# Rotary half swap on TensorE, first weights split ahead of a load, and squares summed on GpSimd: three edits of a two-block transformer kernel

## The chip, the cores and the metric

The kernel runs on one core of a Trainium2 chip. The metric is the device time of one execution in microseconds (us), lower is better. The core has the engines TensorE (PE, and PEld for its weight loads), VectorE (DVE), ScalarE (ACT), GpSimd (POOL) and SyncE (SP, which issues the DMA transfers).

## The reference, cut to what matters

Two blocks of two layers each work on one sequence of 256 tokens of width 1024, all in float32. The pieces that the change touches:

```python
def rms_norm(x, g):
    y = x32 * lax.rsqrt(jnp.mean(x32 * x32, axis=-1, keepdims=True) + EPS)
    return (y * g).astype(x.dtype)

def apply_rope(x, cos, sin):           # halves of 32 in a head of 64
    x1, x2 = x[..., :half], x[..., half:]
    return concatenate([x1 * c - x2 * s, x2 * c + x1 * s], axis=-1)

# first block, each layer: mod = silu(c) @ w_ada[l] + b_ada[l]
h = rms_norm(x, g_norm1[l]) * (1.0 + sc1) + sh1
u = h @ w_in[l] + b_in[l]              # q_lat, kv_lat, k_rope, ... by columns
# ... latent attention (with rope on a part of q and k), stick-breaking attention
x = x + gt1 * (merged @ w_out[l])
h = rms_norm(x, g_norm2[l]) * (1.0 + sc2) + sh2    # then a gated feed-forward part

# second block, each layer: the same frame; 8 + 8 query heads and 2 + 2 key heads of 64,
# each normed per head and, on the 256 main tokens, rotated by rope; the 256 context
# tokens go through the same projections without rope; then 16 experts of 32 tokens each.
q = apply_rope(rmsnorm(p_q, qg), cos, sin)
x = x + gt1 * latent_mixer(...)        # ends with merged @ w_out
x = x + gt2 * expert_choice_ffn(modulate(rmsnorm(x, g_ffn), sh2, sc2), ...)
```

## The kernel before, in words

Activations lie feature-major: 128 features on the partitions, 256 tokens along the free dimension, eight such tiles for the width of 1024. A float32 product is made of three products of rounded parts: `wsplit` (lines 227 and 228) casts a weight tile to its high part on ScalarE and subtracts to get the low part on VectorE, and `mm3` (line 245) multiplies high by high, high by low and low by high. One 128-column tile of a projection is thus 24 matmuls of 256 columns. Small products (sums over the partitions, attention of the first block) are plain float32 matmuls; on the page each of them is two rows.

The order of the program text is not the order on the engines: a scheduler under the tile framework places each instruction on its in-order engine, and buffers are given out by tags with a fixed number of slots. The PSUM tags are `mm` (2 slots), `dd` (3) and `acc` (3). SP issues all loads of weights in one queue.

What the change and the prediction touch:

- **Start of the program** (`body`, `prep`, `cols1`, `first_layer`). The six parts of the first adaptive vector come from loads of 1 MB of `w_ada`, eight of which are taken by TensorE at the start (line 406). When the last is in, the first norm (lines 483, 491) makes the parts `hh` and `hl`, and the first projection runs on weights of `w_in` (`fm2`, line 245). That first load of `w_in` stands behind the eight of `w_ada`.
- **Norm statistics** (`Stats.add`, line 113). Behind each of the eight 128-feature tiles of an out projection (`out_proj`, line 751 adds the tile to x), ScalarE squares the tile and TensorE adds its sum over the partitions by a float32 matmul with a matrix of ones. In the mixers of the second block a second small matmul (line 116) makes router logits beside it. There are five out projections: two layers of the first block, context and main tokens of the second block's first layer, main tokens of its last.
- **`rsqrt`** (line 303 and around): logarithm and exponential on ScalarE, then one Newton step on VectorE; line 303 makes the scaled input for that step on VectorE.
- **`rope`** (lines 766 to 768): four GpSimd instructions, each on 32 partitions, multiply a quarter by the sines and write it to the other half of its head; VectorE multiplies by the cosines (767) and adds (768). It runs twice in each layer of the first block and ten times in each mixer of the main tokens (two key and eight query tiles), 24 in all, which makes 96 GpSimd rows.
- **`head_norm`** (lines 909 to 917 of the second block's heads): square on ScalarE, scaling by the gain on VectorE (line 910), a float32 matmul with a block matrix (line 912), `rsqrt`, `rope`. Line 926 or 1017 multiplies by the norm, lines 1020 and 1021 split.

The main mixer of a layer runs: keys and values of both branches, four query tiles of branch one, attention of branch one (lines 957 to 985), four query tiles of branch two, attention of branch two, then projections and the out projection, and then the experts (line 1272), whose 192 MB of weights follow in the same load queue.

Of the kernel before, what the change touches and what calls it, by code (L numbers as in the profile page):

```python
# [17 lines left out]
P = 128  # L18
# [28 lines left out]
    [("ident", P), ("slot", 1), ("freq", 1), ("eps", 1), ("halfpi", 1), ("one", 1), ("sign", 1), ("ones", P), ("mask_m", P)],  # L47
# [16 lines left out]
def shape_constants():  # L64
# [8 lines left out]
    c["sign"][:, 0] = sign  # L73
    c["ntri"][:] = -(p[:, None] >= p[None, :]).astype(np.float32)
# [26 lines left out]
class Stats:  # L101
    def __init__(self, kernel, x, bank=None, proj=None):
        self.kernel, self.x, self.ps, self.bank, self.proj = kernel, x, None, bank or kernel.ad, proj

    def add(self, k):
        kn = self.kernel
        if self.ps is None:
            kn.use_table("ln_exp")
            bank = self.bank()
            self.ps, self.pl = bank[:, :S], bank[:, S:2 * S]  # L110
        sq = kn.k1([P, S])
        kn.act(sq, self.x[:, k], AF.Square)
        i = kn.nc.tensor.matmul(self.ps, kn.c("ones"), sq, start=k == 0, stop=k == KT - 1, skip_group_check=True)  # L113
        if self.proj:
            w, e = self.proj
            j = kn.nc.tensor.matmul(self.pl[e], w[:, k], self.x[:, k], start=False, stop=k == KT - 1,
                                    skip_group_check=True)
            if k == 0:
                kn.order(i, j)
# [6 lines left out]
class Kernel:  # L126
# [164 lines left out]
    def rsqrt(self, ps, n, scale, shape=None, out=None):  # L291
# [11 lines left out]
        nc.vector.tensor_scalar(f(v), ps, scale, EPS, op0=OP.mult, op1=OP.add)  # L303
        self.act(y, y, AF.Exp, scale=-0.5)
        nc.vector.tensor_tensor(u, y, y, op=OP.mult)
# [206 lines left out]
    def cols1(self, l):  # L512
# [27 lines left out]
        if l == 0:  # L540
            for r, (n, o, _) in zip(rows, sets):
                self.rows_out(r, n, o)
        yield c1, c2, c3

    def first_layer(self, l, cols, mod, then, r):
# [14 lines left out]
        w = self.wload(w_in, 0, KT, 0, 256)  # L560
        ql = self.k2([P, 2, S])
        pq = self.mm((P, S))
        jobs = [(self.dd(), self.wsplit1(w[:, :, j * P:(j + 1) * P], [P, KT, P])) for j in range(2)]
        self.fm2(jobs, h)
        if l == 0:
            self.const_rest()
        for j in range(2):
# [159 lines left out]
        st = Stats(self, x)  # L727
# [29 lines left out]
    def rope(self, q, n, cos, sin):  # L757
# [6 lines left out]
        for a in range(0, P, 32):  # L764
            src, dst = slice(a, a + 32), slice(a ^ 32, (a ^ 32) + 32)
            nc.gpsimd.tensor_tensor(u[dst], q[src], sin[src], op=OP.mult)  # L766
        nc.vector.tensor_tensor(o, q, cos, op=OP.mult)
        nc.vector.tensor_tensor(o, o, u, op=OP.add)
# [137 lines left out]
    def head_norm(self, ps, g, rot, gain):  # L906
# [3 lines left out]
        nc.vector.tensor_scalar(q, ps, g, gain, op0=OP.mult, op1=OP.mult)  # L910
# [7 lines left out]
    def kv(self, l, s, h, c, kk, vv):  # L918
# [5 lines left out]
        for br, w in enumerate(ws):  # L924
            q, r = self.head_norm(jobs[br][0], c[:, 65 + 2 * br:66 + 2 * br], s == 0, 1.0)
# [73 lines left out]
    def mixer(self, l, s, x, mod, cols, kk, vv, h, side=None, steps=None):  # L999
# [5 lines left out]
        outs = {}  # L1005
        for br in range(2):
            half = [self.wload(w_in, 4 * f, 4, 512 + 512 * br, 512) for f in range(2)]
            q = self.k8([P, 2, 4, S], F32R)
            for mt in range(4):
# [6 lines left out]
                qq, r = self.head_norm(ps, c[:, 64 + 2 * br:65 + 2 * br], s == 0, 0.125)  # L1016
# [77 lines left out]
        st = Stats(self, x, proj=(wr, e))  # L1094
# [320 lines left out]
def body(tc, io, out, consts, n1=DEPTH, n2=DEPTH):  # L1415
    with ExitStack() as ctx:
# [7 lines left out]
        def prep(i):  # L1424
# [7 lines left out]
            if ns == 1:  # L1432
# [77 lines left out]
```

## Time and profile before

| what | value |
|---|---|
| runs | 2777.68, 2778.06, 2783.66 us; median 2778.06 |
| the profiled execution | 2779.97 us, its span 2778.0 us |
| busy share of the span | PE 93%, PEld 66%, DVE 51%, ACT 38%, POOL 5% |
| TensorE clock | 0.976 of full speed on average |
| loads | 742.59 MB, 267 GB/s on average |

The busy share of PE is a mean over stages with different limits. Matmuls are pipelined, so a row's duration is longer than the step to the next row: a 256-column row of line 245 lasts 0.28 us and the next follows 0.117 us later at full clock.

### The profile page before, as it was taken

What the parts mean: (1) busy time and instruction counts of PE and PEld (TensorE: products, weight loads), DVE (VectorE), ACT (ScalarE), POOL (GpSimd) and SP (SyncE); (2) the same over time, 40 slices, a digit from 0 to 9 for tenths busy, and PEclk for the clock granted to TensorE, in tenths of its full rate; (3) what the DMA queues carried; (4) which work ended last, traced back from release to release, by engine and by line L of the source; (5) the groups of instructions that cost most, each with busy time, mean ns of one, the idle gap of its engine ahead of it and who ended that gap; (6) DMA issues with size and microseconds to landing.
All of it is one profiled execution on the core that took longest, in us unless ns stands there. A gap on an engine that the chain in (4) does not pass through costs nothing.

```text
span 2778.0 us, 45247 instructions
## 1 busy us (share of the span) xinstructions
PE 2573.3 (93%) x18732; PEld 1828.8 (66%) x18732; DVE 1409.1 (51%) x2667; ACT 1050.6 (38%) x1986; POOL 132.7 (5%) x155
## 2 busy tenths in 40 slices
PE   7998999999999999889999999999889998878886
PEld 5898998888998689768984333333667994222222
DVE  5989977767778855797552011010598562000001
ACT  3564555555556644556452000001466442000000
POOL 0100000000000000120011000000031001000000
PEclk8999999999999999999999999999999999999998
DMA  8788854677555488423656999999623766999999
GB/s 315 238 317 287 322 175 155 221 281 249 178 193 191 153 272 263 135 76 114 182 179 235 361 410 400 425 379 407 242 77 114 228 220 257 424 425 424 424 425 320
DMA packets 315003, 742.59 MB, mean 267 GB/s; under 512 B 16214, under 2 KB 212782, under 8 KB 275118
## 3 DMA queue, kind: packets, MB, share of 16 engines
q1 hardware_dynamic: 313710, 738.66, 72.0%
q8 instruction: 147, 2.41, 0.3%
q10 hardware_dynamic: 1088, 1.05, 0.1%
q14 instruction: 58, 0.48, 0.1%
HBM read 738.61 MB, written 1.05 MB: 266 GB/s over the span
## 4 chain that ended last, share of the span: by engine, by line
PE 72%; DMA 15%; DVE 8%; ACT 3%; issue 1%; POOL 1%; SPq 1%; DVEq 0%; ACTq 0%; POOLq 0%
PE dd L245 36%; PE acc L1272 11%; PE mm L1272 5%; PE acc L245 3%; DMA k<-in_w_e_down_dram 3%; DMA w<-in_w_e_up_dram 2%; DMA k<-in_w_e_up_dram 2%; DMA w<-in_w_e_down_dram 2%; DMA k<-in_w_e_gate_dram 2%; DMA w<-in_w_e_gate_dram 2%; PE mm L985 2%; PE ad L406 2%; PE ad L113 1%; PE mm L979 1%; DVE wl L228 1%
## 5 line engine op out<-in xcount | busy, mean ns | idle before, releaser
L245 PE MATMUL dd<-hh,wh 128*128 128x256 f32 x2384 | 682.9, 288 | 17.1 <-ACT hh L269 13.6
L228 DVE TENSOR_TENSOR wl<-w,wh 128x1024 fp32r<-128x1024 f32 (+1 forms) x534 | 553.9, 1041 | 270.7 <-ACT wh L227 264.1
L245 PE MATMUL dd<-hh,wl 128*128 128x256 f32 x2384 | 676.9, 285 | 12.7 <-DVE wl L228 12.5
L227 ACT CAST wh<-w 128x1024 fp32r<-128x1024 f32 (+1 forms) x534 | 478.0, 900 | 527.2 <-PE dd L245 389.5
L245 PE MATMUL dd<-hl,wh 128*128 128x256 f32 x2384 | 675.5, 284 | 1.0 <-DVE hl L491 0.8
L245 PEld LDWEIGHTS dd<-hh,wh 128*128 128x128 f32 x2384 | 453.8, 191 | 38.7 <-ACT hh L269 15.1
L245 PEld LDWEIGHTS dd<-hh,wl 128*128 128x128 f32 x2384 | 454.4, 191 | 18.3 <-DVE wl L228 14.7
L245 PEld LDWEIGHTS dd<-hl,wh 128*128 128x128 f32 x2384 | 455.2, 191 | 6.4 <-issue 3.2
L1272 PE MATMUL acc<-w,pt 128*32 128x512 f32 x624 | 222.9, 597 | 30.0 <-DMA w<-in_w_e_up_dram 16.1
L1294 DVE TENSOR_TENSOR wh<-wh,acc 128x512 f32<-128x512 f32 x20 | 13.8, 688 | 450.1 <-PE acc L1272 450.1
L1272 PE MATMUL acc<-k,pt 128*32 128x512 f32 x692 | 224.0, 597 | 8.7 <-DMA k<-in_w_e_up_dram 5.2
L245 PE MATMUL dd<-k,wh 128*128 128x256 f32 x896 | 165.0, 284 | 1.1 <-DVE k L665 0.8
L1272 PE MATMUL acc<-w,k 128*32 128x512 f32 x480 | 160.9, 608 | 0.7 <-ACT pt L1169 0.7
L1272 PE MATMUL acc<-w,wl 128*32 128x512 f32 x396 | 139.8, 600 | 13.9 <-DMA w<-in_w_e_down_dram 13.9
L1272 PE MATMUL acc<-k,wl 128*32 128x512 f32 x432 | 146.7, 600 | 4.6 <-DMA k<-in_w_e_down_dram 4.6
L245 PEld LDWEIGHTS dd<-k,wh 128*128 128x128 f32 x896 | 138.6, 190 | 4.8 <-DVE k L665 1.7
L1272 PE MATMUL acc<-k,k 128*32 128x512 f32 x376 | 133.3, 605 | 0.0
L1272 PEld LDWEIGHTS acc<-w,pt 128*32 128x32 f32 x624 | 45.8, 109 | 131.7 <-issue 69.0
L766 POOL TENSOR_TENSOR k<-k,rope 32x256 f32<-32x256 f32 (+1 forms) x96 | 88.4, 921 | 852.2 <-DVE k L599 460.0
L245 PE MATMUL dd<-k,wl 128*128 128x256 f32 x448 | 126.2, 282 | 2.2 <-DVE wl L228 2.2
L1307 DVE SCALAR_TENSOR_TENSOR x_res<-dd,mod,x_res 128x256 f32<-128x256 f32 x64 | 28.9, 484 | 174.5 <-PE dd L1306 174.4
L1272 PEld LDWEIGHTS acc<-k,pt 128*32 128x32 f32 x692 | 46.3, 109 | 93.7 <-issue 61.6
(357 smaller groups left out, 4444.0 us busy)
## 6 DMA issues: line engine op xcount, KB each, us to landing
w<-in_w_in_dram SPq DMA_DIRECT2D x104, 1024.0 KB
w<-in_w_ada_dram SPq DMA_DIRECT2D x63, 1024.0 KB
w<-in_w_e_gate_dram SPq DMA_DIRECT2D x54, 1024.0 KB
w<-in_w_e_up_dram SPq DMA_DIRECT2D x54, 1024.0 KB
w<-in_w_e_down_dram SPq DMA_DIRECT2D x48, 1024.0 KB
w<-in_w_up_dram SPq DMA_DIRECT2D x44, 1024.0 KB
k<-in_w_e_gate_dram SPq DMA_DIRECT2D x43, 1024.0 KB
k<-in_w_e_down_dram SPq DMA_DIRECT2D x43, 1024.0 KB
```

The source lines that it names most:

```text
L113: i = kn.nc.tensor.matmul(self.ps, kn.c("ones"), sq, start=k == 0, stop=k == KT - 1, skip_group_check=True)
L227: self.nc.scalar.copy(h, src)
L228: self.nc.vector.tensor_tensor(l, src, h.bitcast(F32), op=OP.subtract)
L245: self.last_mm = self.nc.tensor.matmul(ps, a, b, start=first and i == 0, stop=last and i == len(ops) - 1, skip_group_check=group)
L406: nc.tensor.matmul(ad[32 * g:32 * g + 32], cs[:, 2 * c + j], t[:, j, 256 * g:256 * g + 256], start=j == 0 and (c == 0 or not hold), stop=j ...
L766: nc.gpsimd.tensor_tensor(u[dst], q[src], sin[src], op=OP.mult)
L979: nc.tensor.transpose(pp[:, i], e[:, i * P:(i + 1) * P], self.c("ident"))
L985: nc.tensor.matmul(po[64 * f:64 * f + 64], vv[:, kt, P * br + 64 * f:P * br + 64 * f + 64], pt[:, f, i], start=i == 0, stop=i == len(kts) ...
L1272: nc.tensor.matmul(accs[s][n][32 * e:32 * e + 32], lhs(s, 2 * kp + k, e), tiles[e][k][:, 512 * n:512 * n + 512], start=kp == 0 and k == 0, ...
L1294: nc.vector.tensor_tensor(a, a, pu[s][n], op=OP.mult)
L1307: nc.vector.scalar_tensor_tensor(x[:, k], ps, gate[:, k:k + 1], x[:, k], op0=OP.mult, op1=OP.add)
```

## The change

Three edits are joined. First, `rope` makes the swapped halves with one float32 matmul by a signed permutation (`swap`) into a PSUM tile of the tag `mm`, and VectorE multiplies that tile by the sines; GpSimd does nothing there any more. The gain of a head is applied by ScalarE and no longer by VectorE, and so is the scaled input in `rsqrt`. Second, the first load of `w_in` is queued ahead of the eighth load of `w_ada`, and its two column tiles are split right there; the constants and two of three rows of columns change places in the order too. Third, the statistics behind the five out projections (`sums=True`) keep the first and last square as they are, and GpSimd adds squares two to seven into one tile, of which TensorE makes one matmul: three matmuls instead of eight.

```diff
-    [("ident", P), ..., ("ones", P), ("mask_m", P)],
+    [("ident", P), ..., ("ones", P), ("mask_m", P), ("swap", P)],
+    c["swap"][p ^ 32, p] = -1.0
...
 class Stats:
...
-        sq = kn.k1([P, S])
+        if self.sums and k == 1:
+            self.total = sq = kn.t([P, S], "sq", 1)
+        else:
+            sq = kn.k1([P, S])
         kn.act(sq, self.x[:, k], AF.Square)
-        i = kn.nc.tensor.matmul(self.ps, kn.c("ones"), sq, start=k == 0, stop=k == KT - 1, skip_group_check=True)
+        if self.sums and 1 < k < KT - 1:
+            kn.nc.gpsimd.tensor_tensor(self.total, self.total, sq, op=OP.add)
+            sq = self.total
+        if not (self.sums and 0 < k < KT - 2):
+            i = kn.nc.tensor.matmul(self.ps, kn.c("ones"), sq, start=k == 0, stop=k == KT - 1, skip_group_check=True)
...
     def rsqrt(...):
-        nc.vector.tensor_scalar(f(v), ps, scale, EPS, op0=OP.mult, op1=OP.add)
         self.act(y, y, AF.Exp, scale=-0.5)
+        self.act(f(v), ps, AF.Identity, bias=self.c("eps"), scale=scale)
...
+    def first_weights(self, w_in):
+        w = self.wload(w_in, 0, KT, 0, 256)
+        self.ready = [self.wsplit1(w[:, :, j * P:(j + 1) * P], [P, KT, P]) for j in range(2)]
...
     def rope(self, q, n, cos, sin):
-        for a in range(0, P, 32):
-            src, dst = slice(a, a + 32), slice(a ^ 32, (a ^ 32) + 32)
-            nc.gpsimd.tensor_tensor(u[dst], q[src], sin[src], op=OP.mult)
+        turned = self.mm((P, S) if n is None else (P, n, S))
+        nc.tensor.matmul(turned, self.c("swap"), q, start=True, stop=True)
         nc.vector.tensor_tensor(o, q, cos, op=OP.mult)
+        nc.vector.tensor_tensor(u, turned, sin, op=OP.mult)
         nc.vector.tensor_tensor(o, o, u, op=OP.add)
...
-    def head_norm(self, ps, g, rot, gain):
+    def head_norm(self, ps, g, rot):
-        nc.vector.tensor_scalar(q, ps, g, gain, op0=OP.mult, op1=OP.mult)
+        self.act(q, ps, AF.Copy, scale=g)
...
     def prep(i):
-                    for _ in range(KT):
+                    for n in range(KT):
                         k.filler(1)
                         cols = cols or next(g)
+                        if n == KT - 2:
+                            k.first_weights(io["w_in"][0])
...
-    nc = bacc.Bacc("TRN2", target_bir_lowering=False, num_devices=1, dynamic_dma_scratch_size=2048)
+    nc = bacc.Bacc("TRN2", target_bir_lowering=False, num_devices=1, dynamic_dma_scratch_size=512)
```

How the rows stand on the engines, at three places.

**VectorE at the start**, from the copy of the last adaptive sums on (`acc`), with `w` and `wh` the weights of `w_in` and their high part, before:

```order
L413 COPY k_37_233<-acc_188 128x256
L394 TENSOR_TENSOR mod_177<-mm_235,c_26_178 128x2x4
L413 COPY k_44_284<-acc_242 128x256
L394 TENSOR_TENSOR mod_177<-mm_286,c_26_178 128x2x4
L504 SCALAR_TENSOR_TENSOR tiny_309<-mod_177,c_26_178 128x2 x4
L336 COPY c_26_178<-mm_300 128x39
```

and in the change:

```order
L422 COPY k_37_233<-acc_188 128x256
L403 TENSOR_TENSOR mod_177<-mm_235,c_26_178 128x2x4
L237 TENSOR_TENSOR wl_277<-w_274,wh_276 128x1024
L237 TENSOR_TENSOR wl_281<-w_274,wh_280 128x1024
L422 COPY k_49_294<-acc_242 128x256
L403 TENSOR_TENSOR mod_177<-mm_296,c_26_178 128x2x4
```

The two splits of the first weights, which stood behind the norm, stand ahead of the last adaptive copy.

**TensorE at the keys of the main tokens** in the second block's first layer: the end of the key projections, the block sums of the two key heads, and the start of the values, before:

```order
L245 MATMUL dd_13581<-hh_13294,wl_13583 128x256
L912 MATMUL dd_13638<-k_2298_13634,cst 128x256
L912 MATMUL dd_13670<-k_2306_13666,cst 128x256
L245 MATMUL dd_13698<-wh_13700,hh_13294 128x256
L245 MATMUL dd_13698<-wl_13701,hh_13294 128x256
```

and in the change:

```order
L254 MATMUL dd_13579<-hh_13292,wl_13581 128x256
L928 MATMUL dd_13636<-k_2303_13632,cst 128x256
L781 MATMUL mm_13649<-k_2304_13633,cst 128x256
L928 MATMUL dd_13667<-k_2312_13663,cst 128x256
L781 MATMUL mm_13680<-k_2313_13664,cst 128x256
L254 MATMUL dd_13694<-wh_13696,hh_13292 128x256
L254 MATMUL dd_13694<-wl_13697,hh_13292 128x256
```

A swap (L781) stands right behind the block sum (L928) of its head, ahead of the next work on TensorE.

**TensorE in the last part of branch one's attention** (transposes L979, weighted values L985, scores L957), where branch two's second query tile has its block sum (L912) and its third query tile begins (L245), before:

```order
L912 MATMUL dd_14459<-k_2489_14455,cst 128x256
L979 MATMUL mm_14159<-cst,k_2415_14155 128x128 x4
L979 MATMUL mm_14178<-cst,k_2421_14174 128x128 x4
L957 MATMUL acc_14241<-k_1641_10092,k_2330_13784 128x512
L979 MATMUL mm_14191<-cst,k_2425_14187 128x128 x4
L985 MATMUL mm_14197<-pt_14132,k_1645_10096 64x256
L957 MATMUL acc_14241<-k_1642_10093,k_2330_13784 128x512
L957 MATMUL acc_14242<-k_1641_10092,k_2330_13784 128x512
L957 MATMUL acc_14242<-k_1642_10093,k_2330_13784 128x512
L245 MATMUL dd_14483<-hh_13294,wh_14484 128x256
```

and in the change (L995 and L1001 are the transposes and weighted values):

```order
L995 MATMUL mm_14324<-cst,k_2477_14320 128x128 x4
L995 MATMUL mm_14337<-cst,k_2481_14333 128x128 x4
L1001 MATMUL mm_14343<-pt_14278,k_1649_10092 64x256 x8
L781 MATMUL mm_14407<-k_2491_14391,cst 128x256
L928 MATMUL dd_14452<-k_2502_14448,cst 128x256
L781 MATMUL mm_14465<-k_2503_14449,cst 128x256
L254 MATMUL dd_14475<-hh_13292,wh_14476 128x256
L254 MATMUL dd_14475<-hl_13293,wh_14476 128x256
```

The swaps of branch two's first two query tiles, the second block sum and all of the third tile's projection stand behind the attention's last matmul, where before the third projection was strewn into the attention.

## Rows read from the trace of the kernel before

**Rows 1.** The page's part 1: busy time of each engine, share, instructions.

```profile
span 2778.0 us, 45247 instructions
PE 2573.3 (93%) x18732; PEld 1828.8 (66%) x18732; DVE 1409.1 (51%) x2667; ACT 1050.6 (38%) x1986; POOL 132.7 (5%) x155
```

**Rows 2.** Stretches: us, then busy time per engine, PEclk, DMA share, GB/s.

```profile
50.00:110.00 60.00, 53.76 (x390) 50.13 (x389) 54.50 (x84) 32.74 (x60) 12.16 (x9) 0.97 0.64 209
1155.00:1200.00 45.00, 28.23 (x194) 25.72 (x193) 42.98 (x87) 23.15 (x55) 22.58 (x29) 0.91 0.29 94
1200.00:1292.00 92.00, 82.87 (x535) 64.58 (x536) 79.75 (x200) 62.34 (x152) 13.82 (x16) 0.95 0.24 81
2000.00:2040.00 40.00, 30.28 (x188) 27.94 (x188) 35.70 (x72) 24.73 (x59) 14.18 (x21) 0.83 0.40 139
2040.00:2143.00 103.00, 91.28 (x591) 70.24 (x591) 89.02 (x218) 68.39 (x168) 24.14 (x28) 0.97 0.22 72
2300.00:2340.00 40.00, 32.08 (x194) 17.37 (x196) 12.96 (x30) 15.08 (x29) 10.64 (x12) 0.83 0.43 158
2340.00:2778.00 438.00, 349.58 (x1680) 99.64 (x1672) 24.62 (x48) 16.54 (x31) 0.00 (x0) 0.98 1.00 408
```

**Rows 3.** Chain that ended last, second out projection: start, us, what.

```profile
645.42 0.69 PE ad L113 x2
646.11 2.80 PE dd L245 x24
648.91 0.70 PE ad L113 x2
```

**Rows 4.** The same chain, out projection of the last mixer.

```profile
2280.87 3.00 PE dd L245 x24
2283.87 0.68 PE ad L113 x2
2284.55 0.54 PE ad L116 x2
```

**Rows 5.** Stretches again, in and behind the out projections of first layer and mixers.

```profile
185.00:230.00 45.00, 44.43 (x357) 42.33 (x356) 44.13 (x74) 24.28 (x38) 0.00 (x0) 1.00 0.93 329
1120.00:1155.00 35.00, 35.00 (x245) 28.35 (x245) 20.89 (x36) 14.77 (x25) 0.00 (x0) 1.00 0.39 123
2267.00:2300.00 33.00, 33.00 (x224) 26.48 (x225) 13.70 (x22) 9.67 (x17) 0.00 (x0) 1.00 0.70 255
```

**Rows 6.** Groups of POOL by shape: busy, mean ns, idle before and releaser.

```profile
L766 POOL TENSOR_TENSOR k<-k,rope 32x256 f32<-32x256 f32 x88 | 76.1, 864 | 843.4 <-DVE k L599 460.0 <-DVE k L910 342.2 <-DVE tiny L974 25.0
L1176 POOL TENSOR_TENSOR k<-x_res,rx 128x256 f32<-128x256 f32 x16 | 12.3, 787 | 219.8 <-DVE rx L308 219.2 <-ACT k L269 0.6
```

**Rows 7.** Groups of DVE by shape, 1155 to 1292 us (one mixer).

```profile
L1021 DVE TENSOR_TENSOR k<-k,k 64x256 fp32r<-64x256 f32 x16 | 9.5, 595 | 0.4
L767 DVE TENSOR_TENSOR k<-k,rope 128x256 f32<-128x256 f32 x10 | 7.0, 703 | 0.0
L305 DVE TENSOR_TENSOR k<-k 128x256 f32<-128x256 f32 x11 | 6.9, 630 | 0.1
L306 DVE SCALAR_TENSOR_TENSOR k<-k,k 128x256 f32<-128x256 f32 x11 | 6.8, 615 | 0.0
L910 DVE TENSOR_SCALAR k<-dd,c 128x256 f32<-128x256 f32 x10 | 4.8, 479 | 0.1
L303 DVE TENSOR_SCALAR k<-dd 128x256 f32<-128x256 f32 x10 | 4.2, 416 | 0.5 <-ACT k L269 0.5
L768 DVE TENSOR_TENSOR k<-k,k 128x256 f32<-128x256 f32 x10 | 4.1, 413 | 0.6 <-POOL k L766 0.6
```

**Rows 8.** Waits of PE: total us, times, longest.

```profile
PE dd L912 <- ACT k L269: 12.8, 15, 1.8
```

**Rows 9.** Timeline of the start: start, us, engine, line, operation, idle before.

```profile
27.52 1.93 PE L406 MATMUL acc<-k,k 128*32 128x256 f32 x16 [0.62 <-DMA k<-in_w_ada_dram]
30.04 1.70 PE L406 MATMUL acc<-k,k 128*32 128x256 f32 x16 [0.59 <-DMA k<-in_w_ada_dram]
33.57 1.27 DVE L483 SCALAR_TENSOR_TENSOR k<-x_res,tiny,rx 128x256 f32<-128x256 f32 x3
39.82 1.21 DVE L228 TENSOR_TENSOR wl<-w,wh 128x1024 fp32r<-128x1024 f32 x1
40.96 0.47 DVE L491 SCALAR_TENSOR_TENSOR hl<-k,mod,hh 128x256 fp32r<-128x256 f32 x1
48.44 1.56 ACT L269 ACTIVATE k<-dd,c 128x256 f32<-128x256 f32 x4
```

More of the change, by code (lines that the diff above doesn't have):

```diff
@@ L46 @@
 CONST_WIDTHS = [
-    [("ident", P), ("slot", 1), ("freq", 1), ("eps", 1), ("halfpi", 1), ("one", 1), ("sign", 1), ("ones", P), ("mask_m", P)],
+    [("ident", P), ("slot", 1), ("freq", 1), ("eps", 1), ("halfpi", 1), ("one", 1), ("sign", 1), ("ones", P), ("mask_m", P), ("swap", P)],
     [("ones_top", P), ("ones_bot", P), ("ntri", P), ("nones", P), ("mask_s", P), ("keep", P)],
@@ L101, with __init__ @@
 class Stats:
-    def __init__(self, kernel, x, bank=None, proj=None):
+    def __init__(self, kernel, x, bank=None, proj=None, sums=False):
         self.kernel, self.x, self.ps, self.bank, self.proj = kernel, x, None, bank or kernel.ad, proj
+        self.sums, self.total = sums, None
     def add(self, k):
@@ L540, in cols1 @@
         if l == 0:
-            for r, (n, o, _) in zip(rows, sets):
-                self.rows_out(r, n, o)
+            turn = [lambda r=r, n=n, o=o: self.rows_out(r, n, o) for r, (n, o, _) in zip(rows, sets)]
+            turn[0]()
+            self.later = turn[1:]
         yield c1, c2, c3
+    def first_weights(self, w_in):
+        w = self.wload(w_in, 0, KT, 0, 256)
+        self.ready = [self.wsplit1(w[:, :, j * P:(j + 1) * P], [P, KT, P]) for j in range(2)]
     def first_layer(self, l, cols, mod, then, r):
@@ L558, in proj @@
             return ps
-        w = self.wload(w_in, 0, KT, 0, 256)
+        if l:
+            self.first_weights(w_in)
         ql = self.k2([P, 2, S])
         pq = self.mm((P, S))
-        jobs = [(self.dd(), self.wsplit1(w[:, :, j * P:(j + 1) * P], [P, KT, P])) for j in range(2)]
+        jobs = [(self.dd(), w) for w in self.ready]
         self.fm2(jobs, h)
@@ L566, in first_layer @@
             self.const_rest()
+            [f() for f in self.later]
         for j in range(2):
@@ L726, in first_layer @@
         g1 = self.half(m[:, 16:24], KT)
-        st = Stats(self, x)
+        st = Stats(self, x, sums=True)
         self.out_proj(io["w_out"][l], (mh, ml), g1, x, st)
@@ L924, in kv @@
         for br, w in enumerate(ws):
-            q, r = self.head_norm(jobs[br][0], c[:, 65 + 2 * br:66 + 2 * br], s == 0, 1.0)
+            q, r = self.head_norm(jobs[br][0], c[:, 65 + 2 * br:66 + 2 * br], s == 0)
             nc.vector.tensor_tensor(q, q, r, op=OP.mult)
@@ L1005, in mixer @@
         outs = {}
+        qg = self.tiny([P, 2])
+        nc.vector.tensor_scalar(qg, c[:, 64:68:2], 0.125, None, op0=OP.mult)
         for br in range(2):
@@ L1015, in mixer @@
                 self.fm(ps, self.wsplit([P, KT, P], parts), h)
-                qq, r = self.head_norm(ps, c[:, 64 + 2 * br:65 + 2 * br], s == 0, 0.125)
+                qq, r = self.head_norm(ps, qg[:, br:br + 1], s == 0)
                 nc.vector.tensor_tensor(qq, qq, r, op=OP.mult)
@@ L1093, in mixer @@
         nc.vector.tensor_tensor(wr, wr, a[:, :, None].to_broadcast([P, KT, N_EXP]), op=OP.mult)
-        st = Stats(self, x, proj=(wr, e))
+        st = Stats(self, x, proj=(wr, e), sums=True)
         self.out_proj(io["w_out_2"][l], mhl, self.half(m[:, 16:24], KT), x, st, side() if side else None)
```

## The prediction

> **What bounds the kernel now.** I read the page's busy shares first: TensorE 93%, VectorE 51%, GpSimd 5% [rows 1]. That says TensorE on the whole, so I cut the span into stretches to see where it is not so [rows 2]. TensorE is idle for 2778.0 - 2573.3 = 204.7 us [rows 1]. Of that, 438.00 - 349.58 = 88.4 us lie in the last experts, where the DMA share is 1.00: loads bound that stage, and only its start can move. The next largest pieces are the two mixers of the main tokens in the second block. In the first, 1155 to 1292 us, TensorE is idle 137 - 28.23 - 82.87 = 25.9 us, in the second, 2000 to 2143 us, 143 - 30.28 - 91.28 = 21.4 us. There the reader should look at VectorE: 42.98 of 45.00 us busy in the first stretch of the first mixer, 35.70 of 40.00 in that of the second [rows 2]. These stretches are VectorE's. The out projections are the opposite: TensorE is busy 35.00 of 35.00 and 33.00 of 33.00 us, with VectorE at 20.89 and 13.70 [rows 5]. So each of the three edits has to be priced in its own stage.
>
> Does time saved upstream reach the end? In the stretch from 2300 us, ahead of the last experts, the DMA share is 0.43 [rows 2]: what fits of their weights is in, and they start when TensorE gets there. I pass everything saved before 2333 us through in full.
>
> **Squares summed on GpSimd.** Each of the five out projections loses five of eight matmuls with ones, 25 in all. In the chain of the first block's second layer, 24 weight matmuls take 2.80 us and the one with ones 0.69 to 0.70 us behind them [rows 3]. In the mixers the same two lines are followed by 0.54 us for the logits [rows 4], which stay. The chain runs through TensorE alone there, so a removed matmul is a removed 0.68 us: 25 x 0.68 = 17.0 us. What could take it back is GpSimd. One sum has the shape of line 1176, 0.787 us [rows 6]; the steps between tiles are 2.8 + 0.7 us or more, so the sum of tile seven is done before square eight is ready, and no matmul waits for it. GpSimd's queue holds nothing else there but, in one mixer, the products of line 1176. The cost that can show is on VectorE, by slowing the weight splits. In four out projections VectorE has room: 35.00 - 20.89 = 14.1 us and 33.00 - 13.70 = 19.3 us [rows 5] against 5 x 0.79 = 3.9 us. In the first layer it has none: 44.13 of 45.00 us [rows 5]. I take off half of that one's gain, 1.7 us. Sum: -15.3 us, with -17.0 and 0 as ends.
>
> Rows first: VectorE's product with the cosines, beside a running GpSimd rotation, takes 0.703 us on average where the addition of the same shape behind it takes 0.413 [rows 7]. The Trainium skill (SBUF — State Buffer, section Who interferes with whom) says that a VectorE instruction with two SBUF inputs contends with a GpSimd instruction that reads SBUF, and that the loser waits for the whole instruction. By that rule the new product, which has one input in PSUM, is free of it, and the 25 new sums can each hold up a weight split. The trace agrees as far as the rotations go; the sums are not in it. By the rule alone the second edit speaks against itself: 25 x 0.787 = 19.7 us of VectorE at most, which would cancel the gain only where VectorE is as full as TensorE; it is the first rival below.
>
> **The swap on TensorE.** Removed: 96 GpSimd rows, four of 0.864 us to a head tile [rows 6]. Added: 24 float32 matmuls and 24 VectorE products. From VectorE go the scaling (line 910, 0.479 us) and the scaled input (line 303, 0.416 us) to ScalarE, which is busy 23.15 of 45.00 us in the full stretch [rows 2] and so hides them. Per mixer VectorE loses 4.8 + 4.2 us for these [rows 7] and what the rotation cost its neighbours: against 0.413 us of line 768, line 767 is 10 x 0.29 = 2.9 us too long, line 305 11 x 0.217 = 2.4, line 306 11 x 0.202 = 2.2 [rows 7]; line 1021 is slowed too, which I leave as margin. It gains ten products, 10 x 0.413 = 4.1 us. Net 4.8 + 4.2 + 7.5 - 4.1 = 12.4 us of VectorE. Six of the ten heads lie in the full stretch, which gives 7.4 us there; the other four lie beside attention, where VectorE is 79.75 of 92.00 us and TensorE 82.87 [rows 2], and I count 0.6 us for them.
>
> TensorE's side: the nearest row for a swap is the 0.69 us of the matmul with ones [rows 3], ten to a mixer, 6.9 us. The 25.9 us of idle time cover it if they lie where the swaps lie; they do for the first six. A swap stands right behind its head's block sum in TensorE's queue (second place above), and it waits for ScalarE's scaled copy as the block sum waits for the square, 12.8 / 15 = 0.85 us each time [rows 8]. The next projection is queued behind it. And the tag `mm` has two slots that attention uses: the third place above shows two swaps and a projection of 24 matmuls, 2.80 us, moved behind branch one's attention. Ends for a mixer: -12.4 us if VectorE sets the pace throughout, +13.8 us if TensorE does (10 x 0.69 + 10 x 0.41 for the second ScalarE step, by line 768's size, + 2.80). I take -8.0, nearer to VectorE, because that engine is 96% busy where most heads lie. Two mixers: -16.0 us.
>
> In the first block's two layers TensorE is busy 53.76 of 60.00 us around the rotations and VectorE 54.50 [rows 2]. Two swaps add 0.69 and, at twice the columns, 1.4 us; the idle 6.2 us can shrink by some 3. I take -0.5 us a layer, -1.0 us, with +2 and -3 a layer as ends. The heads of the context tokens exchange two VectorE steps for two ScalarE steps, and `rsqrt` elsewhere the same: nothing, since both engines are under 60% on average [rows 1].
>
> **First weights ahead of the last adaptive load.** The adaptive pieces reach TensorE 30.04 - 27.52 = 2.52 us apart [rows 9], so 1 MB of `w_in` in front delays the last by that and the norm's first row from 33.57 to 36.1 us. Now the norm runs to 40.96 + 0.47 = 41.43 us, 7.86 us, with one split of 1.21 us inside [rows 9]; without it 6.65 us, to 42.7 us. The projection follows tile by tile and ends six matmuls later, at some 44 us, where today its first reader on ScalarE starts at 48.44 us [rows 9]. That is -4.4 us; the third split is still behind the norm, so I take -3.5. Ends: -5.5, and +2.5 if only the delay is left. Nothing waits for the two smaller rows that change places.
>
> **The sum.** -15.3 - 16.0 - 1.0 - 3.5 = -35.8 us. The profiled execution took 2779.97 us, so it would be 2744.2; the median of the runs stands 1.9 us below it, so I forecast **2742 us**. Its own range is 2730 to 2753.
>
> **The rivals.**
>
> *The sums give back what they save.* VectorE's splits, held up by the sums, become the limit of the out projections, or the projections' tiles arrive no sooner because the scheduler fills the time with adaptive work on VectorE. For it: VectorE's 44.13 of 45.00 us in the first layer; against it: the other four. -15.3 becomes 0: 2757 us.
>
> *VectorE's time comes out whole.* The mixers lose 12.4 us each and the slowed line 1021 some more, say 16 each, down to TensorE's own work. For it: 25.9 and 21.4 us of idle time; against it: swaps and projection behind attention. 2742 - 16 = 2726 us.
>
> *TensorE's queue becomes the limit of the mixers.* Each swap with its wait stands in front of the next projection, and VectorE's relief buys nothing: 2 x 13.8 + 2 x 2.0 = +31.6 us, less 15.3 and 3.5, gives +12.8 us: 2791 us, slower. It decides once a head costs more than (15.3 + 3.5) / 24 = 0.78 us net. For it: 0.69 us of matmul alone is near that; against it: TensorE idles 16.8 us of the 45.00 where six heads lie.
>
> *The change doesn't do what it says.* The removed matmuls are gone from TensorE's order and the rotations from GpSimd's; only the start could fail, if the weights land late and the copy of the last adaptive sums, queued behind both splits on VectorE, waits: +2.5 for -3.5, 2748 us, inside the forecast's range.
>
> **How the numbers follow.** The forecast has 0.52, sums given back 0.20, VectorE's time whole 0.15, TensorE's queue 0.08, and 0.05 stays for effects of the new order in stages that the change does not name, half of them slower. The range 2722 to 2766 us holds the first three with the unknown ends around them. A measurement of this kernel tells about 0.2% from no change, 5.6 us: 2772.5 to 2783.6 us count as the same. Faster 0.87, the same 0.05, slower 0.08.
>
> **What would show it.** Right: pieces of 24 weight matmuls follow each other without 0.7 us between them in five places of each out projection's chain; line 306's and 305's means fall to about 0.41 us; VectorE's busy time in a main mixer falls by 12 us and TensorE's idle time by more than 7; the first projection's reader starts at about 45 us; the stretch of the last experts keeps its 438 us. Wrong: TensorE's waits for ScalarE ahead of the swaps add up to more than 10 us, or weight splits in the out projections take 2 us instead of 1.2, or the last experts get longer by what was saved ahead of them.

## The result and the profile after

The changed kernel takes **2748.5 us** (median of 4 runs, 2744.7 to 2751.0) against 2778.8 us for the kernel before on the same chip: a ratio of 0.9886, 95% interval 0.9868 to 0.9904. It is 30.3 us faster, where 2742 us and 36 us were forecast; the time lies inside the range. The first rival, at 2757 us, is hardly farther from it than the forecast, so the sum has to be judged term by term.

The page's part 1 of the changed kernel (an execution of 2746.6 us) answers to [rows 1]:

```profile
span 2744.8 us, 45167 instructions
PE 2556.2 (93%) x18730; PEld 1813.3 (66%) x18730; DVE 1361.8 (50%) x2607; ACT 1079.1 (39%) x2073; POOL 74.9 (3%) x84
```

The span is 33.2 us shorter, 3 more than the medians say: the profiled executions stand 1.1 us over (before) and 2.0 us under (after) the medians. TensorE's busy time gives 17.1 us of it and its idle time 16.1 (204.7 to 188.6 us). To see where, I followed marks that both programs have, by their times in the two traces (us):

| Mark | before | after | gained since the start |
|---|---|---|---|
| first layer: first matmul with ones behind the first projection | 49.3 | 48.2 | 1.1 |
| first layer: last matmul with ones of the key heads (L667, now L683) | 89.8 | 83.4 | 6.4 |
| first layer: end of attention | 175.1 | 167.5 | 7.6 |
| first out projection, first to last matmul with ones | 217.6 to 238.9 | 211.2 to 233.2 | 5.7 |
| second layer: end of attention | 571.8 | 569.2 | 2.6 |
| second out projection, with the sums behind it | 635.1 to 666.8 | 631.9 to 661.2 | 5.6 |
| context mixer's out projection | 1122.0 to 1150.7 | 1114.8 to 1142.3 | 8.4 |
| first main mixer: end of attention | 1293.9 | 1279.0 | 14.9 |
| its out projection, to the last logits | 1421.0 to 1460.8 | 1406.4 to 1442.7 | 18.1 |
| second main mixer: end of attention | 2143.9 | 2114.2 | 29.7 |
| its out projection, to the last logits | 2272.0 to 2301.6 | 2241.6 to 2268.3 | 33.3 |
| first matmul of the last experts | 2321.7 | 2288.5 | 33.2 |
| end | 2778.0 | 2744.8 | 33.2 |

The last experts keep their 456.3 us, so what is saved ahead of them reaches the end. The five out projections change by +0.7, -2.4, -1.2, -3.5 and -2.9 us, together **-9.3** where -15.3 was forecast. From the block sums to the end of attention the main mixers give 6.6 and 11.1 us, **-17.7** for -16.0. The remaining 6.2 us are a balance: the first block's front, which was costed at 1 us, gives about 5 in the first layer and takes some 3 in the second, and the head, the stretch ahead of the context mixer's out projection and the joints between the stages give the others.

The two mixers as stretches (us, then busy time per engine, PEclk, DMA share, GB/s), first before, then after; they begin and end at the same marks:

```profile
1156.00:1293.90 137.90, 112.46 (x735) 91.04 (x735) 122.55 (x286) 84.66 (x206) 36.40 (x45) 0.94 0.25 85
1994.60:2143.90 149.30, 127.86 (x822) 103.64 (x821) 130.00 (x298) 96.94 (x232) 38.33 (x48) 0.93 0.29 96
```

```profile
1147.70:1279.00 131.30, 113.69 (x751) 90.54 (x751) 106.16 (x275) 91.27 (x226) 2.44 (x5) 0.96 0.27 89
1976.00:2114.20 138.20, 125.02 (x837) 101.36 (x836) 112.73 (x284) 104.55 (x257) 4.05 (x8) 0.99 0.31 104
```

VectorE's busy time falls by 16.4 and 17.3 us, TensorE's idle time by 7.8 (25.4 to 17.6) and 8.3 us (21.4 to 13.2). In the second mixer TensorE's busy time falls as well, by 2.8 us with more matmuls in it, and the granted clock goes from 0.93 to 0.99 of 2.4 GHz: an engine that idles less ran on the higher level for more of the stretch.

Groups of DVE by shape in the first mixer, 1147 to 1279 us, answer to [rows 7]. The root's two products and the product with the cosines are down to 0.42 to 0.44 us, and the rows of the two moved steps are gone:

```profile
L1039 DVE TENSOR_TENSOR k<-k,k 64x256 fp32r<-64x256 f32 x16 | 6.7, 420 | 1.0 <-ACT k L1038 0.5
L314 DVE TENSOR_TENSOR k<-k 128x256 f32<-128x256 f32 x11 | 4.6, 421 | 1.3 <-ACT k L278 1.2
L315 DVE SCALAR_TENSOR_TENSOR k<-k,k 128x256 f32<-128x256 f32 x11 | 4.6, 418 | 0.1
L782 DVE TENSOR_TENSOR k<-k,rope 128x256 f32<-128x256 f32 x10 | 4.4, 439 | 0.0
L783 DVE TENSOR_TENSOR k<-mm,rope 128x256 f32<-128x256 f32 x10 | 4.2, 417 | 0.1
```

**What the sums lost.** The waits of TensorE over the whole program (total us, times, longest) have a row that was not there before:

```profile
PE ad L122 <- POOL sq L119: 6.2, 5, 2.6
```

One wait in each out projection: by stretches 2.6, 1.3, 1.3, 0.5 and 0.5 us. The chain of the second out projection shows how it comes about (start, us, what), beside [rows 3]:

```profile
632.59 13.71 PE dd L254 x118
646.31 1.43 issue
647.73 1.05 ACT wh L236
648.78 0.32 ACT k L278
...
649.24 1.39 POOL sq L119
650.63 0.04 issue
650.68 0.70 PE ad L122 x2
651.38 1.18 PE dd L254 x10
```

The matmul of the sum stands in TensorE's queue with ten matmuls of the eighth tile behind it. It needs the seventh tile's square, which ScalarE makes behind the next weights' cast (1.05 us), and then a GpSimd sum of 1.39 us, not 0.79. The reader should not take the 4.4 us from 646.31 to 650.68 as idle: TensorE goes on with matmuls that the chain doesn't list and waits 1.28 us at the end.

### The profile page after: what moved, and what is told of

Read it like the earlier page. It is cut to its first block, busy times and chain, and to the rows that moved or that the text cites. A ratio compares the mean times of both kernels' runs of the same rounds, so it can differ in the third digit from the quotient of the medians.

```text
span 2744.8 us, 45167 instructions
## 1 busy us (share of the span) xinstructions
PE 2556.2 (93%) x18730; PEld 1813.3 (66%) x18730; DVE 1361.8 (50%) x2607; ACT 1079.1 (39%) x2073; POOL 74.9 (3%) x84
## 3 DMA queue, kind: packets, MB, share of 16 engines
q10 hardware_dynamic: 1088, 1.05, 0.1%
HBM read 738.67 MB, written 1.05 MB: 269 GB/s over the span
## 4 chain that ended last, share of the span: by engine, by line
PE 72%; DMA 16%; DVE 5%; ACT 4%; issue 1%; SPq 1%; POOL 0%; ACTq 0%; DVEq 0%; POOLq 0%
PE dd L254 36%; PE acc L1290 11%; PE mm L1290 5%; PE acc L254 3%; DMA k<-in_w_e_down_dram 3%; DMA w<-in_w_e_up_dram 3%; DMA k<-in_w_e_up_dram 2%; DMA k<-in_w_e_gate_dram 2%; DMA w<-in_w_e_down_dram 2%; DMA w<-in_w_e_gate_dram 2%; PE mm L1001 2%; PE ad L415 2%; ACT k L278 1%; ACT wh L236 1%; PE mm L995 1%; PE acc L973 1%
## 5 line engine op out<-in xcount | busy, mean ns | idle before, releaser
L254 PEld LDWEIGHTS dd<-hh,wh 128*128 128x128 f32 x2384 | 451.3, 190 | 35.8 <-ACT hh L278 13.2
L1290 PE MATMUL acc<-w,pt 128*32 128x512 f32 x624 | 223.4, 601 | 30.3 <-DMA w<-in_w_e_up_dram 16.4
L1317 ACT COPY wl<-dd 128x512 f32<-128x512 f32 x24 | 13.2, 591 | 242.7 <-PE dd L1316 242.7
```

The costliest lines, as they stand in the source:

```text
L254: self.last_mm = self.nc.tensor.matmul(ps, a, b, start=first and i == 0, stop=last and i == len(ops) - 1, skip_group_check=group)
L1290: nc.tensor.matmul(accs[s][n][32 * e:32 * e + 32], lhs(s, 2 * kp + k, e), tiles[e][k][:, 512 * n:512 * n + 512], start=kp == 0 and k == 0, ...
L1317: nc.scalar.copy(tt[:, 4 * n:4 * n + 4], ps)
```

## The experiments

Each was timed in 5 rounds beside the kernel before; times are medians, and the interval is that of the ratio to the kernel before. That kernel's own median was 2779.8 us beside the first four (the three edits alone and the late sum), 2780.3 beside the next four (moves undone, moves alone, the late sum without the first layer, and on VectorE), 2780.5 beside the rest, and 2778.8 beside the changed kernel, so a difference to the changed kernel carries 1 or 2 us from that alone. The last line of the change, the smaller `dynamic_dma_scratch_size`, goes along in every kernel below except the first weights alone and the moves alone; no run has it alone.

### The three edits, one at a time

**Sums alone.** The kernel before with

```diff
...
+        if self.sums and 1 < k < KT - 1:
+            kn.nc.gpsimd.tensor_tensor(self.total, self.total, sq, op=OP.add)
+            sq = self.total
+        if not (self.sums and 0 < k < KT - 2):
...
```

> The kernel before with only the squares' sums on GpSimd (25 matmuls with ones fewer). Theory A (TensorE waits for the last sum, 6.2 us in all in the changed kernel, and the first layer gives nothing, because VectorE has no room there): -9 us against the kernel before, about 2770 us, with waits of TensorE for the sums of 6 us in the five out projections together. Theory B (the sums give the whole forecast, and the loss comes from the other two edits' new order): -15 us, about 2764 us, with waits under 2 us.

Measured: 2772.7 us, -7.1 us, ratio 0.9975 (0.9964 to 0.9985). TensorE waits 5.8 us in five waits for the sums, and the out projections change by +0.3, -1.2, -1.2, -3.6 and -2.9 us. Theory A holds: the loss belongs to this edit, not to the new order around it.

**Swap and moves alone.**

```diff
-            nc.gpsimd.tensor_tensor(u[dst], q[src], sin[src], op=OP.mult)
+        nc.tensor.matmul(turned, self.c("swap"), q, start=True, stop=True)
+        nc.vector.tensor_tensor(u, turned, sin, op=OP.mult)
...
-        nc.vector.tensor_scalar(f(v), ps, scale, EPS, op0=OP.mult, op1=OP.add)
+        self.act(f(v), ps, AF.Identity, bias=self.c("eps"), scale=scale)
-        nc.vector.tensor_scalar(q, ps, g, gain, op0=OP.mult, op1=OP.mult)
+        self.act(q, ps, AF.Copy, scale=g)
```

> The kernel before with only the rotary swap as a matmul, and the scaling and the scaled input moved to ScalarE. Theory A (stage by stage as in the changed kernel: the two main mixers -18, the first layer's front -5, the second layer's front +2, the context mixer -2): -23 us, about 2756 us. Theory B (the forecast's terms, -16 and -1): -17 us, about 2762 us; then part of what the stages show belongs to one of the other edits. In both the rotations' rows on GpSimd are gone and the chain of the first layer's front no longer runs through GpSimd.

Measured: 2758.9 us, -20.9, ratio 0.9929 (0.9917 to 0.9941). It is between the two theories, nearer to A.

**First weights alone**, with the two rows of columns that change places in the order.

```diff
-        w = self.wload(w_in, 0, KT, 0, 256)
+        if l:
+            self.first_weights(w_in)
...
+                        if n == KT - 2:
+                            k.first_weights(io["w_in"][0])
```

> The kernel before with only the first weights ahead of the last adaptive load. Theory A (the delay of the last adaptive piece eats most of what the earlier splits save): -1 us, about 2778 us, the norm's first row 4 us later than before, the first projection's reader 1 us earlier. Theory B (the forecast): -3.5 us, about 2775 us, norm's first row 2.5 us later. Theory C (the delay is the transfer of other constants that the rotary swap adds in front, not this edit): the norm's first row only 2.5 us later here, against 4.1 in the changed kernel.

Measured: 2774.0 us, -5.8, ratio 0.9983 (0.9974 to 0.9991); the norm's first row at 37.00 us, 3.4 later than before. Theory C explains little: most of the 4.1 us come without the swap's constants. The total is above A and fits B or more, but one trace does not settle where it comes from: against before, the first projection's mark is 1.2 us earlier, the start of the first out projection 3.2, that of the context mixer's 3.7, and the end of the first mixer's attention 2.1. The three medians add up to -33.8 us.

### The wait of the sum

```diff
-            sq = self.total
-        if not (self.sums and 0 < k < KT - 2):
+        if self.sums and k == KT - 1:
+            kn.nc.tensor.matmul(self.ps, kn.c("ones"), self.total, start=False, stop=False, skip_group_check=True)
+        if not (self.sums and 0 < k < KT - 1):
```

> The changed kernel, with the matmul of the sum taken from behind the seventh tile to behind the eighth, so that TensorE has the whole last tile to do while GpSimd ends the sum. Theory A (the lost part is TensorE's wait for the last sum, 2.6 + 1.3 + 1.3 + 0.5 + 0.5 = 6.2 us): -3.5 to -6 us against the changed kernel, about 2744 us, and these waits gone; in the first layer some of it stays lost, because VectorE is full there. Theory B (what is lost is VectorE's time, held up by GpSimd's sums): 0 to -1 us, about 2748 us.

Measured: 2742.5 us, 6.0 us under the changed kernel; ratio 0.9868 (0.9855 to 0.9881). The intervals of the two ratios still touch, so the trace has to carry it. Of five waits one is left, in the first layer:

```profile
PE ad L121 <- POOL sq L119: 1.9, 1, 1.9
```

The out projections change by -0.2, -4.1, -3.2, -4.6 and -4.1 us against before, together -16.2: the forecast's -15.3 is there once four of the five waits are gone. GpSimd's sums are as slow as ever (1.193 us for 1.190), so theory B, VectorE held up, is not what cost four of the five.

**The first layer.** The same with the first block's first out projection as before:

```diff
-        st = Stats(self, x, sums=True)
+        st = Stats(self, x, sums=l > 0)
```

> The kernel of the late sum (2742.5 us), with the first layer's and the second layer's flag set so that the first out projection keeps its eight matmuls with ones. Theory A (in the first layer VectorE is full, TensorE's matmuls are hidden, and the sums slow the adaptive sums on VectorE from 1.28 to 1.52 us, ten times): 1 to 3 us faster, about 2740.5 us. Theory B (TensorE sets the pace there once it no longer waits): 2 to 3.4 us slower, about 2745 us.

Measured: 2741.0 us, ratio 0.9860 (0.9847 to 0.9874). With five matmuls more the first out projection takes 21.4 us, 21.2 with the sums: TensorE has 1.9 us less to do there (20.20 to 18.32 us busy) and waits 1.9 us for the sum instead. The total is not resolved from the late sum's.

**Sums on VectorE.**

```diff
-            kn.nc.gpsimd.tensor_tensor(self.total, self.total, sq, op=OP.add)
+            kn.nc.vector.tensor_tensor(self.total, self.total, sq, op=OP.add)
```

> The kernel of the late sum (2742.5 us), with the sums on VectorE. 25 sums of about 0.42 us are added to VectorE and none runs on GpSimd. Theory A (contention between the two engines costs the out projections time): VectorE's adaptive sums go back from 1.52 to 1.28 us in the first layer, 2.4 us, against 5 x 0.42 = 2.1 us added: within 1 us in all, and the other four out projections unchanged. Theory B (VectorE waits in its queue for ScalarE's square in front of the next split): 0.5 to 1 us for each sum that waits, 3 to 10 us slower, about 2748 us.

Measured: 2741.6 us, ratio 0.9862 (0.9847 to 0.9877): theory A. Groups of DVE in the first out projection, the late sum first (205 to 234 us), then with the sums on VectorE:

```profile
L468 DVE SCALAR_TENSOR_TENSOR k<-k,cc,k 128x1024 f32<-128x1024 f32 x9 | 13.9, 1543 | 0.0
L238 DVE TENSOR_TENSOR wl<-w,wh 128x1024 fp32r<-128x1024 f32 x10 | 12.1, 1213 | 0.0
```

```profile
L238 DVE TENSOR_TENSOR wl<-w,wh 128x1024 fp32r<-128x1024 f32 x10 | 12.2, 1218 | 0.0
L468 DVE SCALAR_TENSOR_TENSOR k<-k,cc,k 128x1024 f32<-128x1024 f32 x9 | 11.5, 1277 | 0.0
L119 DVE TENSOR_TENSOR sq<-sq,k 128x256 f32<-128x256 f32 x5 | 2.1, 418 | 0.1
```

The five sums cost VectorE 2.1 us, and its nine adaptive sums give back 9 x 0.266 = 2.4 us. From the first to the last matmul with ones this out projection takes 19.0 us, for 21.2 with the late sum, but the layer's end comes no earlier (442.7 and 442.1 us). Behind the out projection, from 230 to 250 us, VectorE is now busy for 19.29 of 20 us where it was 17.70 with the late sum, so its adaptive work may hold the layer there; no run shows that by itself.

**Both together.**

```diff
+            kn.nc.vector.tensor_tensor(self.total, self.total, sq, op=OP.add)
...
+        st = Stats(self, x, sums=l > 0)
```

> The kernel of the late sum, sums on VectorE, and none in the two layers of the first block except the second: the first out projection keeps its eight matmuls with ones. If the two variants' small gains (1.5 and 0.9 us against the late sum) are real and apart, about 2740 us; if they are one and the same, or noise, 2741 to 2742.5 us.

Measured: 2742.8 us, ratio 0.9871 (0.9855 to 0.9886). Nothing is added. The late sum in any of these forms, 2741 to 2743 us, is what the runs found faster than both kernels.

### What the mixers gain from

**Moves undone, swap kept.**

```diff
...
-        self.act(q, ps, AF.Copy, scale=g)
+        nc.vector.tensor_scalar(q, ps, g, gain, op0=OP.mult, op1=OP.mult)
...
-        self.act(f(v), ps, AF.Identity, bias=self.c("eps"), scale=scale)
+        nc.vector.tensor_scalar(f(v), ps, scale, EPS, op0=OP.mult, op1=OP.add)
```

> The changed kernel with the scaling of the head and the scaled input of the root put back on VectorE (the swap stays on TensorE). Theory A (VectorE's busy time is what the mixers gain from): 0.479 + 0.416 us of VectorE come back for each of ten heads, 9 us to a mixer, of which some 0.6 count, as 17 us less VectorE time went with 7 and 11 us less span: about 9 to 11 us slower than the changed kernel, 2758 us. Theory B (the gain is the rotation: its waits and what it slowed on VectorE): within 2 us of the changed kernel, about 2749 us. Theory C (with both moves ScalarE sets the pace, since it stands in the chain of the first mixer in the changed kernel): 1 to 4 us faster.

Measured: 2753.8 us, ratio 0.9900 (0.9886 to 0.9914), 5.2 us over the changed kernel by the medians, with intervals that overlap. Between A and B; for theory C, a faster kernel, nothing speaks.

**Moves alone**, on the kernel before (the lines above, the other way round):

```diff
...
-        nc.vector.tensor_scalar(q, ps, g, gain, op0=OP.mult, op1=OP.mult)
+        self.act(q, ps, AF.Copy, scale=g)
...
```

> The kernel before with only the two moves from VectorE to ScalarE, the rotation still on GpSimd. Theory A (VectorE's busy time is the gain): 9 to 11 us faster than before, about 2769 us. Theory B (the rotation is the gain): within 2 us of before, about 2779 us.

Measured: 2768.8 us, -11.4, ratio 0.9958 (0.9945 to 0.9971): theory A. In its first mixer GpSimd still rotates for 36.55 us, and VectorE's busy time is down from 122.55 to 114.68:

```profile
1156.00:1290.70 134.70, 114.39 (x731) 92.58 (x732) 114.68 (x265) 92.12 (x228) 36.55 (x45) 0.94 0.27 87
```

**Swap alone**, on the kernel before:

```diff
...
-            nc.gpsimd.tensor_tensor(u[dst], q[src], sin[src], op=OP.mult)
+        nc.tensor.matmul(turned, self.c("swap"), q, start=True, stop=True)
+        nc.vector.tensor_tensor(u, turned, sin, op=OP.mult)
...
```

> The kernel before with only the rotation as a matmul with the swap matrix; scaling and scaled input stay on VectorE. Theory A (the swap and the moves to ScalarE relieve the same VectorE time, so together they gave 20.9 us where the moves alone gave 11.4): 15 to 17 us faster than before, about 2764 us. Theory B (the two gains are apart and add up): 9.5 us faster, about 2771 us.

Measured: 2762.9 us, -17.7, ratio 0.9937 (0.9925 to 0.9950): theory A. The stretch of its first mixer has almost the same VectorE time as with the moves alone:

```profile
1153.00:1286.90 133.90, 116.57 (x755) 92.20 (x755) 113.72 (x296) 85.72 (x207) 2.52 (x5) 0.96 0.26 87
```

Alone they give 11.4 and 17.7 us, together 20.9. Both are bought with the same thing, VectorE's time, and what is over once VectorE no longer sets the pace is not paid twice. The mixers show it: from the block sums to the end of attention the swap alone takes 133.5 and 139.8 us (137.7 and 149.4 before), and the seven kernels with both edits, the changed one among them, take 131.2 to 134.2 and 138.1 to 140.4, though VectorE has some 7 us less to do in each mixer.

**Each swap twice.**

```diff
-        nc.tensor.matmul(turned, self.c("swap"), q, start=True, stop=True)
+        for _ in range(2):
+            nc.tensor.matmul(turned, self.c("swap"), q, start=True, stop=True)
```

> The changed kernel with each swap matmul issued twice, the second over the first: 24 more matmuls, about 0.7 us each, 16.7 us of TensorE. Theory A (TensorE's idle time in the mixers, 17.6 and 13.2 us, covers the swaps): 0 to 5 us slower than the changed kernel, about 2751 us. Theory B (each swap stands on TensorE's path, the rival of TensorE's queue): 14 to 17 us slower, about 2764 us.

Measured: 2756.1 us, ratio 0.9915 (0.9901 to 0.9928), 7.6 us over the changed kernel: between the theories, a little under half of the 16.7 us. The trace tells where it is paid. The first mixer's attention ends 14.3 us earlier than before, as good as the changed kernel's 14.9. The stretch behind it, from there to the out projection, is longer, 135 us for 129; first the changed kernel, then this one:

```profile
1275.00:1404.00 129.00, 128.75 (x1106) 127.02 (x1106) 79.01 (x129) 64.98 (x101) 2.97 (x4) 1.00 0.60 176
```

```profile
1275.00:1410.00 135.00, 134.74 (x1147) 132.90 (x1146) 80.40 (x132) 67.84 (x106) 2.96 (x4) 1.00 0.59 176
```

TensorE is full in both, with 41 matmuls more in the second. The swaps took idle time in which the changed kernel had done projections ahead, and these are made up for later. Behind the second mixer's attention it is the same, 131.9 us for 127.4. A swap is hidden where it runs and half paid behind it.

### The head

```diff
...
-                    for n in range(KT):
+                    for _ in range(KT):
                         k.filler(1)
                         cols = cols or next(g)
-                        if n == KT - 2:
-                            k.first_weights(io["w_in"][0])
```

> The kernel of the late sum (2742.5 us) with the first weights back behind the last adaptive load, split behind the norm. Theory A (what the first projection shows, some 2 us, is what the head edit is worth): 1.5 to 3 us slower, about 2745 us. Theory B (worth what it gave alone, 5.8 us): about 2748 us. Theory C (worth nothing, its time alone was noise of the start): within 1 us, about 2742.5 us.

Measured: 2743.3 us, ratio 0.9865 (0.9851 to 0.9878), 0.8 us over the late sum: theory C as far as these runs can tell. Alone the same edit gave 5.8 us. What it is worth stays open between nothing and these 5.8 us.

## Why the prediction was right, and where its steps failed

That the sum came near is in part luck. In the traces, where 33.2 us stand for the forecast 35.8, the out projections and the head are 8.4 us short of their terms, and the mixers, the first block and stretches that had no term give 5.8 us more than theirs.

**Out projections, -15.3 forecast, -9.3 measured.** The step that failed is "the sum of tile seven is done before square eight is ready, and no matmul waits for it". It priced the sum at 0.787 us and asked when the sum would be ready against the next square. The first half of the sentence held (in the chain above the sum ends at 650.63 us, and the matmul of the eighth square starts at 653.93). It should have asked when TensorE gets to the matmul that reads the sum, which stood amid the eighth tile's matmuls. The late sum shows that this one place was worth 16.2 - 9.3 = 6.9 us, 4.3 of them in the waits that went (6.2 to 1.9); what makes up the other 2.6 stays open. The late sum's -16.2 comes near -15.3 by two errors: the first layer gave 0.2 us where 1.7 were left in the sum, and the other four gave 16.0 where 13.6 were forecast. In the changed kernel the first layer even lost 0.7 us.

**The main mixers, -16.0 forecast, -17.7 measured.** The mechanism is right: VectorE set the pace where the heads lie, as either edit alone shows. The size is right by two errors that nearly cancel. VectorE's relief was put too low (12.4 us, measured 16.4 and 17.3, since line 1021, left as margin, also fell from 0.595 to 0.420 us in 16 products, 2.8 us), and the share of it that becomes time too high (8.0 of 12.4, which is 0.65; measured 0.40 and 0.64). The rival in which VectorE's time comes out whole asked for 16 us a mixer; 6.6 and 11.1 came. What is left is TensorE's wait for ScalarE: in the first mixer its waits for VectorE fall from 14.7 to 1.1 us, and those for ScalarE grow from 11.0 to 16.5. Two rows of the changed kernel have nearly all of it:

```profile
PE acc L973 <- ACT k L278: 8.5, 3, 6.5
PE dd L928 <- ACT k L278: 7.4, 7, 2.1
```

In the second mixer ScalarE has 11.1 of 13.2 us of TensorE's idle time. Whether ScalarE's own work, to which both moves were added, or what ScalarE waits for holds it there, no run shows. It is not TensorE that is full in the mixers: with the swaps doubled they take 130.5 and 137.4 us, no more than the changed kernel's 131.3 and 138.1, and the 7.6 us are paid behind them. The rival of TensorE's queue is refuted by the sign, and hardly any wait stands ahead of the swaps: by their line, TensorE idled 2.1 us for ScalarE and 1.2 for VectorE before all of them together.

**The first block's fronts, -1.0 forecast.** The first layer gave about 5 us (from 1.1 to 6.4 between two marks), the second took 3.1 between its first projection and the end of attention. The swap owns the first: alone it gives 4.7 us between the same two marks, the moves alone 0.1. The step that failed is "the idle 6.2 us can shrink by some 3": it read busy sums where the chain had to be read. In the kernel before, the chain of this stretch runs through eight rotations, 11.2 us together; four of them:

```profile
65.52 0.90 POOL k L766
...
66.48 1.62 POOL k L766
...
75.47 1.26 POOL k L766
...
79.01 2.17 POOL k L766
```

In the changed kernel none of them is left, and TensorE idles 2.1 us in the stretch that answers to the first of [rows 2]:

```profile
50.00:104.00 54.00, 51.86 (x385) 48.57 (x383) 51.27 (x83) 34.70 (x64) 0.00 (x0) 1.00 0.74 243
```

The second layer's loss comes with the swap alone (2.7 us) and with the moves alone (2.6 us), not with the sums (0.1): the order that the scheduler chose for less VectorE work may be the reason, but which row of it costs the time was not tried. The stretch ahead of the context mixer's out projection, costed at nothing, gave 1.6 us; the sums alone lose 1.2 us there, so this is not resolved.

**The head, -3.5 forecast, -1.1 at the first projection.** The timeline of the start, after, beside [rows 9]:

```profile
28.47 1.78 PE L415 MATMUL acc<-k,k 128*32 128x256 f32 x16 [0.70 <-DMA k<-in_w_ada_dram]
33.72 1.93 PE L415 MATMUL acc<-k,k 128*32 128x256 f32 x16 [3.47 <-DMA k<-in_w_ada_dram]
37.63 1.26 DVE L492 SCALAR_TENSOR_TENSOR k<-x_res,tiny,rx 128x256 f32<-128x256 f32 x3
43.44 0.88 DVE L500 SCALAR_TENSOR_TENSOR hl<-k,mod,hh 128x256 fp32r<-128x256 f32 x2
47.30 1.56 ACT L278 ACTIVATE k<-dd,c 128x256 f32<-128x256 f32 x4
```

The delay was 5.25 - 2.52 = 2.7 us against the piece ahead, near the 2.5 forecast. That piece was itself 0.95 us later than before. In the traces of four kernels that leave the head as it was (sums, swap with moves, moves, swap), the mark at 49.3 us stands 0.4 to 1.5 us later, so one trace cannot tell an effect of 1 us there. All fourteen traces together can: the projection's first reader starts at 45.5 to 47.3 us in the eight kernels with this edit and at 48.4 to 50.0 us in the six without it, 2.7 us apart by their means, which is three quarters of the forecast 3.5. In the changed kernel's own trace the reader comes 3.3 us after the 44 us of the forecast. Of these, 1.5 us are the norm's first row, at 37.63 and not 36.1 us. The norm takes 37.63 to 44.32, 6.7 us, as forecast. The step that failed is "ends six matmuls later, at some 44 us", which costs the rest: the chain has 25 more matmuls in 3.0 us from 43.71 us on, because TensorE ran at half its clock, 1.2 GHz, while the norm's tiles came, and needed 4.86 us for the 20 before:

```profile
36.00:43.00 7.00, 5.62 (x23) 4.80 (x24) 6.07 (x21) 3.65 (x8) 0.00 (x0) 0.50 1.02 369
43.00:47.00 4.00, 4.00 (x34) 4.00 (x34) 2.61 (x7) 1.02 (x3) 0.00 (x0) 0.92 1.07 395
```

"I pass everything saved before 2333 us through in full" is not shown for this term: the late sum with and without the edit has its first reader at 45.79 and 48.68 us, 2.9 apart, but the end of the first layer's attention at 166.3 and 167.1 us, and the medians are 0.8 us apart. Where the rest goes stays open.

**The signs.** Right: no 0.7 us pieces between the weight matmuls but the first and the last two, means near 0.41 us in the root's products, TensorE's idle time down by more than 7 us in each mixer, VectorE's busy time by more than the 12 us, splits at 1.22 us (two of 1.75 us in the first main mixer's, as before), the last experts unchanged. Wrong: the first reader at 47.30 us and not 45.

## What to carry to other kernels

Where work is taken off a busy engine and handed to another, the price is set by the place in the busy engine's queue of the instruction that reads the result: move that one behind work that is ready anyway, here one tile later for 6 us. Two edits that relieve the same engine are not added, since 11.4 and 17.7 us made 20.9. For a stretch in which two engines are nearly full, read the chain before the busy sums: eight small rows on an engine that is 5% busy were the way to 5 us.

## What the runs showed of the hardware

Which engine pays when a GpSimd sum and a VectorE instruction with two SBUF inputs overlap depends on which began first. The sums' durations (least, median, most) and two meetings in the timeline:

```profile
L119 POOL TENSOR_TENSOR sq<-sq,k x25: 715/1380/1606, 214.8 to 2262.4; 128x256 f32<-128x256 f32 x25
```

```profile
217.76 1.21 DVE L237 TENSOR_TENSOR wl<-w,wh 128x1024 fp32r<-128x1024 f32 x1
218.43 1.13 POOL L119 TENSOR_TENSOR sq<-sq,k 128x256 f32<-128x256 f32 x1 [2.08 <-ACT k L278]
218.89 1.76 DVE L467 SCALAR_TENSOR_TENSOR k<-k,cc,k 128x1024 f32<-128x1024 f32 x1
...
643.23 1.23 DVE L237 TENSOR_TENSOR wl<-w,wh 128x1024 fp32r<-128x1024 f32 x1 [0.54 <-ACT wh L236]
643.65 1.39 POOL L119 TENSOR_TENSOR sq<-sq,k 128x256 f32<-128x256 f32 x1 [1.42 <-ACT k L278]
```

At 643 us the split began first, keeps its 1.23 us, and the sum ends 0.58 us behind it, 1.39 us instead of 0.72. At 218 us the sum, itself begun behind a split and at 1.13 us longer for it, began 0.46 us ahead of the adaptive product, which takes 1.76 us where it took 1.28 without sums. The Trainium skill (SBUF — State Buffer, section Who interferes with whom) says that the order of issue decides who blocks; the trace agrees in these two meetings. The forecast had used that page for VectorE's loss alone; but only 5 of the 25 sums took 0.72 to 0.74 us, the other 20 took 0.99 us or more, and that is part of TensorE's wait.
